# A hybrid encoder layer on one core: the fourth renewed block's remainder taken on GpSimd instead of VectorE

## The chip, the cores and the metric

The kernel runs on one core of a Trainium2 chip. A core has a matrix engine (TensorE, PE in the profile, with its weight loads as PEld), three engines for elementwise work (VectorE = DVE, ScalarE = ACT, GpSimd = POOL) and SyncE (SP), which here only issues transfers between main memory and the on-chip buffer (SBUF). Each engine carries out its own instructions strictly in order and waits at the first one whose inputs are not there. Matmul results go to eight banks of accumulator memory (PSUM), which DVE and ACT read.

The metric is the time of one execution in microseconds (us) on the device. Before the change it is 2638.22 us, the median of three runs (2640.26, 2638.22 and 2636.32).

## The reference, cut to what matters

```python
def hybrid_layer(x, norm_mix_w, w_in, ...):
    h = rmsnorm(x, norm_mix_w)
    proj = einsum("btd,dc->btc", h, w_in)
    u_b, u_c, u_h, z, xbc, dt_raw = split(proj, SPLITS)
    y_a = short_conv_mixer(u_b, u_c, u_h, short_conv_w)     # y = B * conv3(C * h)
    y_b = ssd_mixer(z, xbc, dt_raw, ...)                    # conv, chunked scan, gate, norm
    x = x + einsum("btc,cd->btd", concat([y_a, y_b]), w_out)
    h = rmsnorm(x, norm_mlp_w)
    hid = square(relu(einsum("btd,df->btf", h, w_up)))
    return x + einsum("btf,fd->btd", hid, w_down)

def reference(x, ...):          # x: 1 x 2048 x 1024 float32, one layer, d_ff 4096
    return rmsnorm(hybrid_layer(x, ...), final_norm_w)
```

## The kernel before, in words

**Three matmuls for one.** All products are float32. A block of activations is kept as two halves: `uh`, the value rounded by a cast on ACT, and `ul`, the remainder (value minus `uh`), a subtraction on DVE. Weights are split in the same way into `whi` and `wlo` (`split_w`, L98 to L102: cast on ACT at L100, remainder on DVE at L101). A product is then uh·whi + ul·whi + uh·wlo (L281, L282, L283). A matmul works on a 128x512 tile of activations.

**Seven products for eight.** The four large products (input projection, output projection, MLP up and MLP down) are done in pairs of output columns with seven block products instead of eight; `chain` (L250) issues them in the order b11, t1, t2, b21, t3, b22, t4, twelve matmuls each where four blocks are summed. Their activations are not only the four blocks but sums of them: each of four input groups k = 0 to 3 has four *places* i = 0 to 3. `WHERE` (L193) says which product reads which place: b11 and t1 read place 0, t2 and b21 place 1, t3 and b22 place 2, t4 place 3. Places 0 to 2 are 128x1024 (two tiles), place 3 is 128x512. Products accumulate in the banks px, py and pw, and the next product on a bank waits for the copy that takes the last one out: pw starts from a copy of px after b11 (L288, ACT); t3 goes into px only after ACT has copied t2's result away (`s2<-px`, L746 in the projection, L890 in the MLP).

**Renewing the places.** Three times a product's whole set of places gives way to the next set, which was stored in main memory. It happens inside the last pair that uses the old set: as soon as a place's last product of that pair is issued, the new blocks of this place are cast and their remainders taken, while the later products of the pair still read the other places. `refresh` (L424) does so in the projection's first half, at the end (new blocks `rb` loaded from `hm_d`; called site A below) and at the end of the MLP's first half (`rb` from `hn_d`; site C). `refill` (L979) does so at the end of the MLP's second half, for the first step of the down product (`rh` from `hid_d`; site D). Both call `settle` (L348) after t1, b21, b22 and t4 with i = 0, 1, 2, 3, and right behind it issue the loads of the following place. Those loads go into a ring of four buffers (`uraw`, L201), one for each k, so the load of place i+1 of group k waits until cast and remainder of place i of group k have read the buffer. A fourth use (site B, L1589 and L1598, entry of the MLP) settles places 0 and 1 from tiles that are in SBUF already, with no load behind it. Elsewhere (`stow` at L866, `refill` of one group during the down product) `settle` gets one group only, so k is 0 there.

**What sets the order.** Python code is run once to record the instructions; a scheduler, which goes by its own estimates of durations, then decides for each engine the order in which they stand. So a change of one instruction's engine can move others. SP issues every load and store of these places in one queue: one that must wait holds all behind it. At site D this queue also carries the weights of the down product (`wraw<-w_down`, L972), the stores of the hidden blocks (`hid_d<-...`, L880 and L881) and the sixteen loads of the tiles to which the down product is added (`acc<-x1_d`, L997); an addition on DVE (L1037) frees a bank of the down product once its `acc` tile has landed. GpSimd has next to nothing to do in this kernel: copies of two or three columns for the convolutions, and nine multiplications at the very end (L1133).

Of the kernel before, what the change touches and what calls it, by code (L numbers as in the profile page):

```python
# [11 lines left out]
F32 = mybir.dt.float32  # L12
F32R = mybir.dt.float32r
AF = mybir.ActivationFunctionType
ALU = mybir.AluOpType
# [25 lines left out]
def trunk(ctx: ExitStack, tc: tile.TileContext, x, w_in, w_dt, w_out, w_up, w_down, cvec, hrow, out):  # L41
    nc = tc.nc
# [37 lines left out]
        out=tri, in_=tri, compare_op=ALU.is_ge, fill=0.0, base=0, pattern=[[1, P]], channel_multiplier=-1  # L80
# [115 lines left out]
    class Seven:  # L196
# [149 lines left out]
            return got  # L346

        def settle(self, places, i, got):  # L348
            for p, t in zip(places, got):
                p[i] = self.place(i)  # L350
                t = t[:, 0:1] if i == 3 else t
                nc.scalar.copy(p[i][0], t)  # L352
                nc.vector.tensor_tensor(out=p[i][1], in0=t, in1=p[i][0].bitcast(F32), op=ALU.subtract)

        def last_sums(self):
            for p, t4 in zip(self.places, self.t4s):
# [1309 lines left out]
```

## Time and profile before

| | |
|---|---|
| three runs | 2640.26, 2638.22, 2636.32 us; median 2638.22 |
| profiled execution | 2635.81 us, span 2633.6 us, mean granted TensorE clock 0.997 |
| instructions on DVE / on POOL | 2634 / 98 |
| main memory | 537 MB moved, mean 204 GB/s |

The profile is of one further execution; its span is the time from its first to its last instruction, 2.2 us less than its own time. "Busy" is the share of the span in which an engine works. The chain that ended last is followed back from the last instruction and says, for each stretch of the span, which engine or wait it hung on. A row of the timeline has the start, the duration, the engine and line, the operation with output<-inputs and shape, and in brackets how long the engine had been idle and which instruction or transfer ended that. SPq rows are transfers as SP issues them: their duration is the issuing, not the transfer.

### The profile page before, as it was taken

Reading aid. Unit: us, or ns where it says so; the run is one execution under the profiler, and the core shown is the slowest. Engines: PE = TensorE matmul, PEld = TensorE weight load, DVE = VectorE, ACT = ScalarE, POOL = GpSimd, SP = SyncE. Lnnn points to the kernel's source line nnn. Section 1 sums busy time; section 2 is a strip of 40 time slices with the busy share of each in tenths; the row PEclk is TensorE's granted clock in tenths of the full one; section 3 lists DMA queues with packets and bytes.
Section 4 is the critical chain, followed back from the end, with each engine's and each line's share of the span. In section 5 each row is a group of like instructions: output and inputs, shape, how many; then the busy total and the mean of one; then the engine's idle time right before and its main releaser. Section 6 shows DMA issues by size and latency. Waiting matters only on the chain.

```text
span 2633.6 us, 33784 instructions
## 1 busy us (share of the span) xinstructions
PE 2603.1 (99%) x12136; PEld 2142.1 (81%) x12136; DVE 1919.1 (73%) x2634; ACT 1456.4 (55%) x2211; POOL 55.6 (2%) x98
## 2 busy tenths in 40 slices
PE   9999999999999999999999999999999999999998
PEld 7888888788888888787888888888887888888887
DVE  7977867777778777768677775644448877888985
ACT  6654345776667675857336555655555444444443
POOL 0010000000000000000000000000000000000001
PEclk9999999999999999999999999999999999999999
DMA  3645735555555587867656786765558544665762
GB/s 147 205 168 190 273 144 197 187 165 172 175 169 164 162 283 255 264 210 228 204 195 238 264 314 235 281 211 200 187 197 288 159 150 153 213 208 166 250 208 77
DMA packets 252168, 536.97 MB, mean 204 GB/s; under 512 B 26208, under 2 KB 93024, under 8 KB 252000
## 3 DMA queue, kind: packets, MB, share of 16 engines
q1 hardware_dynamic: 251856, 534.29, 60.7%
q8 instruction: 95, 1.56, 0.2%
q14 instruction: 73, 0.60, 0.1%
q10 hardware_dynamic: 144, 0.52, 0.1%
HBM read 354.89 MB, written 179.83 MB: 203 GB/s over the span
## 4 chain that ended last, share of the span: by engine, by line
PE 65%; issue 25%; ACT 4%; DMA 4%; DVE 2%; POOL 0%; SPq 0%; POOLq 0%; DVEq 0%; ACTq 0%
PE px L281 10%; PE px L282 9%; PE px L283 9%; PE py L281 5%; PE py L282 5%; PE py L283 5%; PE pm L113 4%; PE pm L114 4%; PE pm L115 4%; PE pw L281 2%; PE pw L282 2%; PE pw L283 2%; PE yd L1315 1%; PE yo L1312 1%; ACT dec L1292 1%
## 5 line engine op out<-in xcount | busy, mean ns | idle before, releaser
L281 PE MATMUL px<-uh,whi 128*128 128x512 f32 x1672 | 656.2, 392 | 8.3 <-DVE acc L1037 3.8
L283 PE MATMUL px<-uh,wlo 128*128 128x512 f32 x1672 | 651.6, 390 | 0.0
L282 PE MATMUL px<-ul,whi 128*128 128x512 f32 x1672 | 651.4, 390 | 0.0
L281 PEld LDWEIGHTS px<-uh,whi 128*128 128x128 f32 x1672 | 314.3, 188 | 81.1 <-DVE acc L1037 5.0
L101 DVE TENSOR_TENSOR wlo<-wraw,whi 128x1024 fp32r<-128x1024 f32 x214 | 222.7, 1041 | 203.6 <-ACT whi L100 203.4
L283 PEld LDWEIGHTS px<-uh,wlo 128*128 128x128 f32 x1672 | 314.2, 188 | 66.2 <-issue 0.2
L100 ACT CAST whi<-wraw 128x1024 fp32r<-128x1024 f32 x214 | 194.3, 908 | 313.8 <-PE px L282 224.2
L282 PEld LDWEIGHTS px<-ul,whi 128*128 128x128 f32 x1672 | 314.4, 188 | 63.5
L100 ACT CAST whi<-s 128x1024 fp32r<-128x1024 f32 x210 | 220.1, 1049 | 229.1 <-PE py L282 90.7
L281 PE MATMUL py<-uh,whi 128*128 128x512 f32 x836 | 327.3, 392 | 4.3 <-DVE acc L1037 3.1
L282 PE MATMUL py<-ul,whi 128*128 128x512 f32 x836 | 325.8, 390 | 0.0
L283 PE MATMUL py<-uh,wlo 128*128 128x512 f32 x836 | 325.5, 390 | 0.0
L101 DVE TENSOR_TENSOR wlo<-s,whi 128x1024 fp32r<-128x1024 f32 x210 | 255.5, 1217 | 73.1 <-ACT whi L100 71.5
L113 PE MATMUL pm<-uh,whi 128*128 128x512 f32 (+1 forms) x648 | 251.0, 388 | 0.1
L114 PE MATMUL pm<-ul,whi 128*128 128x512 f32 (+1 forms) x648 | 248.2, 383 | 0.3 <-DVE ul L211 0.2
L115 PE MATMUL pm<-uh,wlo 128*128 128x512 f32 (+1 forms) x648 | 247.9, 383 | 0.0
L281 PEld LDWEIGHTS py<-uh,whi 128*128 128x128 f32 x836 | 156.9, 188 | 39.1 <-DVE acc L1037 3.5
L283 PEld LDWEIGHTS py<-uh,wlo 128*128 128x128 f32 x836 | 157.0, 188 | 33.0 <-DVE wlo L101 0.2
L282 PEld LDWEIGHTS py<-ul,whi 128*128 128x128 f32 x836 | 157.0, 188 | 32.1
L352 ACT CAST uh<-rh 128x1024 fp32r<-128x1024 f32 (+1 forms) x128 | 120.5, 944 | 82.1 <-PE py L283 61.9
L281 PE MATMUL pw<-uh,whi 128*128 128x512 f32 x418 | 163.3, 391 | 0.7 <-ACT pw L288 0.7
L283 PE MATMUL pw<-uh,wlo 128*128 128x512 f32 x418 | 162.8, 389 | 0.0
(241 smaller groups left out, 3794.4 us busy)
## 6 DMA issues: line engine op xcount, KB each, us to landing
hid_d<-e SPq DMA_DIRECT2D x96, 512.0 KB, 3.9
rh<-hid_d SPq DMA_DIRECT2D x96, 512.0 KB, 4.4
wraw<-w_in SPq DMA_DIRECT2D x68, 512.0 KB, 3.8
wraw<-w_down SPq DMA_DIRECT2D x104, 256.0 KB, 3.5
wraw<-w_up SPq DMA_DIRECT2D x48, 512.0 KB, 4.3
dec<-rd_d SPq DMA_DIRECT2D x32, 512.0 KB, 5.0
wraw<-w_out SPq DMA_DIRECT2D x32, 512.0 KB, 4.7
x_d<-xt SPq DMA_DIRECT2D x64, 256.0 KB, 3.3
```

Of the source, the lines that this page charges most:

```text
L100: nc.scalar.copy(hi, raw)
L101: eng.tensor_tensor(out=lo, in0=raw, in1=hi.bitcast(F32), op=ALU.subtract)
L113: nc.tensor.matmul(out, whi, hi, start=(k == 0), stop=False)
L114: nc.tensor.matmul(out, whi, lo, start=False, stop=False)
L115: nc.tensor.matmul(out, wlo, hi, start=False, stop=(k == nk - 1))
L281: nc.tensor.matmul(p, hi, h[0], start=not seeded and k == 0, stop=False, **kw)
L282: nc.tensor.matmul(p, hi, h[1], start=False, stop=False, **kw)
L283: nc.tensor.matmul(p, lo, h[0], start=False, stop=(k == len(g) - 1), **kw)
L352: nc.scalar.copy(p[i][0], t)
L1292: nc.scalar.activation(dec[:, i], dec[:, i], AF.Relu, bias=t["a"][:, i : i + 1], scale=-1.0)
L1312: nc.tensor.matmul(yo[:, j * L : (j + 1) * L], state[:, j * P : (j + 1) * P], cT, start=True, stop=True)
L1315: nc.tensor.matmul(yd[(i % 2) * 64 : (i % 2) * 64 + 64, (i // 2) * L : (i // 2 + 1) * L], byhead(t["xdt"])[:, i, :], t["dec"][:, i % 2 * 4 ...
```

## The change

In `settle` the remainder of the fourth group (k = 3) is taken by GpSimd instead of VectorE. Cast, shapes and arithmetic are the same; the other three groups stay.

```diff
         def settle(self, places, i, got):
-            for p, t in zip(places, got):
+            for k, (p, t) in enumerate(zip(places, got)):
                 p[i] = self.place(i)
                 t = t[:, 0:1] if i == 3 else t
                 nc.scalar.copy(p[i][0], t)
-                nc.vector.tensor_tensor(out=p[i][1], in0=t, in1=p[i][0].bitcast(F32), op=ALU.subtract)
+                eng = nc.gpsimd if k == 3 else nc.vector
+                eng.tensor_tensor(out=p[i][1], in0=t, in1=p[i][0].bitcast(F32), op=ALU.subtract)
```

The lines behind it move by one (L353 becomes L354, L997 becomes L998). Fourteen instructions go from DVE to POOL. On GpSimd these are the first six of them, four at site A (places 0 to 3) and two at B (places 0 and 1); four each at C and D follow, of the same shapes as at A:

```order
L354 TENSOR_TENSOR ul0_3646<-rb_3616,uh0_3645 128x1024
L354 TENSOR_TENSOR ul1_3708<-rb_3655,uh1_3707 128x1024
L354 TENSOR_TENSOR ul2_3768<-rb_3717,uh2_3767 128x1024
L354 TENSOR_TENSOR ul3_3810<-rb_3777,uh3_3809 128x512
L354 TENSOR_TENSOR ul0_12067<-first_11891,uh0_12066 128x1024
L354 TENSOR_TENSOR ul1_12155<-nb_11892,uh1_12154 128x1024
```

The scheduler also moves other instructions at these sites and nowhere else. No instruction is added or dropped. At site C this is ACT's order before, around the fourth place (`uh3`) of the new blocks; `s5` and `s2` are the copies of t1's and t2's results, `whi_14755` is a later weight:

```order
L352 CAST uh3_14663<-rb_14637 128x512
L100 CAST whi_14755<-wraw_14706 128x1024
L352 CAST uh3_14667<-rb_14639 128x512
L352 CAST uh3_14671<-rb_14641 128x512
L890 COPY s5_14725<-py_14712 128x512
L890 COPY s2_14739<-px_14691 128x512
L896 ACTIVATE e0_14688<-pw_14704 128x512
L352 CAST uh3_14675<-rb_14643 128x512
```

The same stretch on ACT with the change:

```order
L352 CAST uh3_14663<-rb_14637 128x512
L891 COPY s5_14725<-py_14712 128x512
L100 CAST whi_14755<-wraw_14706 128x1024
L352 CAST uh3_14667<-rb_14639 128x512
L352 CAST uh3_14671<-rb_14641 128x512
L352 CAST uh3_14675<-rb_14643 128x512
L891 COPY s2_14739<-px_14691 128x512
L897 ACTIVATE e0_14688<-pw_14704 128x512
```

The cast of the last renewed block (`uh3_14675`) stands ahead of the copy `s2<-px` now, and behind it before. At site A the two were in this order already; there the last cast (`uh3_3809`) and a 128x1024 weight cast (`whi_3947`) change places. ACT at site A before:

```order
L352 CAST uh3_3805<-rb_3775 128x512
L100 CAST whi_3947<-wraw_3853 128x1024
L352 CAST uh3_3809<-rb_3777 128x512
L746 COPY s5_3886<-py_3873 128x512
L746 COPY s2_3915<-px_3838 128x512
```

and with the change:

```order
L352 CAST uh3_3805<-rb_3775 128x512
L352 CAST uh3_3809<-rb_3777 128x512
L100 CAST whi_3947<-wraw_3853 128x1024
L747 COPY s5_3886<-py_3873 128x512
L747 COPY s2_3915<-px_3838 128x512
```

So the weight cast now lies between the last block's cast and the two copies. PE at site A takes t4 of the ending pair in one piece ahead of the next pair's b11, where before five matmuls of b11 came first; at site D it does the same with all twelve of b11.

At site D, SP's queue before, behind the last load of the fourth place (`wraw_17166` and `wraw_17167` are weights of the down product's third step, `e0`, `e1` and `t4` the last hidden blocks that are stored):

```order
L989 DMA rh_16953<-hid_d0_3_116 128x512
L972 DMA wraw_17166<-w_down 128x128 x2
L972 DMA wraw_17166<-w_down 128x384
L880 DMA hid_d1_15_144<-e0_16760 128x1024
L880 DMA hid_d1_15_144<-e1_16761 128x1024
L881 DMA hid_d1_15_144<-t4_16989 128x512
L972 DMA wraw_17166<-w_down 128x384
L972 DMA wraw_17167<-w_down 128x128 x2
L972 DMA wraw_17167<-w_down 128x384
L997 DMA acc_17003<-x1_d0_77 128x512
```

The same part of SP's queue with the change:

```order
L990 DMA rh_16953<-hid_d0_3_116 128x512
L881 DMA hid_d1_15_144<-e0_16760 128x1024
L881 DMA hid_d1_15_144<-e1_16761 128x1024
L882 DMA hid_d1_15_144<-t4_16989 128x512
L973 DMA wraw_17051<-w_down 128x256 x2
L973 DMA wraw_17166<-w_down 128x128 x2
L998 DMA acc_17003<-x1_d0_77 128x512
```

The second half of the second step's weights (`wraw_17051`), which stood ahead of the fourth place's loads before, moved behind the store of `t4_16989`. The sixteen `acc` loads now come ahead of the weights in pieces of 384, which follow behind them. On ACT at site D the copy `pw<-px` of the down product's first step moved from right behind the cast of `uh2_16931` to behind the cast of `uh3_16973`, the first block of the fourth place, and the cast of the second step's first weight (`whi_17096`) from ahead of the last two casts of `uh3` to behind them.

## The prediction, made before the changed kernel ran

> **What bounds the kernel.** I read the page's busy line and its chain of waits first, then what PE waited for, then the timelines around the places that the change touches.
>
> ```profile
> PE 2603.1 (99%) x12136; PEld 2142.1 (81%) x12136; DVE 1919.1 (73%) x2634; ACT 1456.4 (55%) x2211; POOL 55.6 (2%) x98
> PE 65%; issue 25%; ACT 4%; DMA 4%; DVE 2%; POOL 0%; SPq 0%; POOLq 0%; DVEq 0%; ACTq 0%
> ```
>
> PE is busy 99% of the span, and the chain that ended last lies on PE or its issuing for 90%. DVE is the fuller of the helpers, yet only 2% of the chain hangs on it. A time saved on DVE is worth something only where PE waits for DVE. The list of PE's waits (engine, line, what it waited for: total us, times, longest) says where:
>
> ```profile
> PE px L281 <- DVE acc L1037: 3.8, 6, 1.4
> PE py L281 <- DVE acc L1037: 3.1, 1, 3.1
> PE px L281 <- ACT s L746: 1.3, 1, 1.3
> ```
>
> The 3.1 us wait (down product) is at site D, the 1.3 us one (ACT's copy in front of t3) at site A. No wait for a remainder `ul` of a renewed block is among the larger ones. So the gain that the change can bring directly is small, and the question is what lies behind the moved instructions.
>
> **The moved instruction.** Fourteen subtractions leave DVE, eleven of 128x1024 and three of 128x512. The groups by form (count | busy us, mean ns of one | idle before) give DVE's price, and the only larger GpSimd instructions of this kernel:
>
> ```profile
> L353 DVE TENSOR_TENSOR ul<-rb,uh 128x1024 fp32r<-128x1024 f32 x24 | 28.4, 1222 | 7.2 <-ACT uh L352 7.2
> L353 DVE TENSOR_TENSOR ul<-rb,uh 128x512 fp32r<-128x512 f32 x8 | 5.4, 690 | 3.0 <-ACT uh L352 3.0
> L1133 POOL TENSOR_TENSOR acc<-acc,rstd 128x256 f32<-128x256 f32 x6 | 4.4, 768 | 12.8 <-ACT rstd L186 12.8
> L1133 POOL TENSOR_TENSOR acc<-acc,rstd 128x512 f32<-128x512 f32 x3 | 4.0, 1363 | 1693.6 <-ACT rstd L186 1693.6
> ```
>
> DVE is relieved of 11 x 1.22 + 3 x 0.69 = 15.5 us. On GpSimd 128x512 costs 1.36 us and each further 256 columns 1.363 - 0.768 = 0.6 us, so a 128x1024 remainder is estimated at 1.36 + 2 x 0.6 = 2.55 us. No row has one: from below it is DVE's 1.22, from above twice 1.36 = 2.7. I take 2.55, which lies near the upper, GpSimd's own row.
>
> Whether GpSimd can start at once is the second unknown. Its small copies show it (first one alone, then one beside DVE, with DVE's rows):
>
> ```profile
> 146.38 0.19 POOL L700 COPY halo<-buf 128x3 f32<-128x3 f32 x1 [32.64 <-DVE buf L749]
> 178.04 2.23 POOL L732 COPY ch<-halo_s 128x2 f32<-128x2 f32 x1 [8.49 <-DVE cacc L704]
> ...
> 177.80 0.69 DVE L214 TENSOR_TENSOR s<-wraw 128x512 f32<-128x512 f32 x1
> 178.40 0.69 DVE L214 TENSOR_TENSOR s<-wraw,s 128x512 f32<-128x512 f32 x1
> 179.00 1.22 DVE L101 TENSOR_TENSOR wlo<-wraw,whi 128x1024 fp32r<-128x1024 f32 x1
> ```
>
> A copy of 0.19 us took 2.23 and ended at 180.27, just behind three back-to-back DVE subtractions (end 180.22). So GpSimd waits here while DVE reads two SBUF tiles, from 0 up to 2.23 - 0.19 = 2.0 us, until DVE has a gap. I take no more than the end of the DVE instruction in progress, because at A and C the remainder that left DVE makes the gap itself; 2.0 us stays as the other end.
> The Trainium skill, "SBUF — State Buffer", section "Who interferes with whom", speaks against this change: a DVE instruction with two SBUF inputs and a GpSimd instruction that reads SBUF exclude each other, and the later one "fully blocks" for the whole instruction. The trace agrees in kind; by the letter of the rule GpSimd would lose at most the rest of one 1.22 us instruction, which is the forecast's case, while the row at 178.04 waited through three.
>
> **Site A.** Rows of ACT, then DVE, SP and PE:
>
> ```profile
> 461.39 1.04 ACT L352 CAST uh<-rb 128x1024 fp32r<-128x1024 f32 x1
> 467.19 1.06 ACT L100 CAST whi<-wraw 128x1024 fp32r<-128x1024 f32 x1 [0.78 <-PE px L282]
> 469.65 0.62 ACT L352 CAST uh<-rb 128x512 fp32r<-128x512 f32 x1 [1.41 <-DMA rb<-hm_d]
> 470.66 0.59 ACT L746 COPY s<-px 128x512 f32<-128x512 f32 x1
> 461.30 2.40 DVE L353 TENSOR_TENSOR ul<-rb,uh 128x1024 fp32r<-128x1024 f32 x2
> 463.72 0.32 SPq L344 DMA_DIRECT2D rb<-hm_d  x1
> 456.55 0.50 PE L281 MATMUL px<-uh,whi 128*128 128x512 f32 x1 [0.88 <-DVE eb L749]
> 461.55 0.50 PE L281 MATMUL py<-uh,whi 128*128 128x512 f32 x1 [0.40 <-ACT eb L784]
> 471.30 0.50 PE L281 MATMUL px<-uh,whi 128*128 128x512 f32 x1 [1.26 <-ACT s L746]
> ```
>
> The cast of place 2, k = 3 ends at 462.43, its remainder on DVE at 463.70, and 0.02 us later SP issues the load of place 3, k = 3 into the freed buffer. ACT then stands still until this block lands (469.65), casts it, makes the two copies, and t3 starts 0.05 us after the second. So load, cast and copy set t3's start. On GpSimd the remainder starts when DVE's k = 2 one ends (461.30 + 1.21 = 462.51) and ends at 465.06: 1.35 us later. In ACT's new order the weight cast of 467.19, which lay inside ACT's wait, comes between the last cast and the copies: 1.06 us. t3 moves by 1.35 + 1.06 = 2.4 us. If the landing does not move with the issue (it took 5.9 us, so other traffic may set it), 1.06 is left; with GpSimd 2.0 us late it is 4.4.
>
> PE's earlier waits here (0.88 and 0.40) can go, since DVE and ACT have less ahead of `eb`; that only lengthens the stall at t3, to 1.26 + 1.28 + 2.4 = 4.9 us. A long stall has a price of its own, as the windows at site D show (window: us, then busy per engine, then PEclk):
>
> ```profile
> 2008.00:2012.00 4.00, 0.90 (x4) 0.43 (x4) 1.77 (x4) 0.41 (x1) 0.00 (x0) 1.00 0.93 270
> 2012.00:2016.00 4.00, 4.00 (x12) 2.86 (x11) 0.68 (x1) 0.00 (x0) 0.00 (x0) 0.57 0.99 361
> 2016.00:2020.00 4.00, 4.00 (x19) 3.29 (x18) 2.18 (x4) 1.06 (x1) 0.00 (x0) 1.00 1.05 387
> ```
>
> After the 3.10 us stall the granted clock was 0.57 for 4 us: 4 x 0.43 = 1.7 us lost. The 1.26 us stall at A has no such trace now. I add 1.7: **A +4.1**, bounds +1.1 and +6.1.
> The Trainium skill, "TensorE: Matmul & The Clock Gate", Part 1, puts the idle window that halves the clock at about 3.4 us; here 3.10 was enough, so the measurement decides, and by either number A's stall pays.
>
> **Site B.** No load hangs on these two remainders.
>
> ```profile
> 1364.00:1383.00 19.00, 19.00 (x85) 15.54 (x84) 15.58 (x18) 9.96 (x11) 0.00 (x0) 1.00 0.31 113
> ```
>
> PE is busy for all 19 us and the places are cast well before use: **B 0**, bounds 0 and +1 (a remainder 1.3 us later in front of its first product).
>
> **Site C.**
>
> ```profile
> 1689.69 1.05 ACT L352 CAST uh<-rb 128x1024 fp32r<-128x1024 f32 x1
> 1695.16 0.58 ACT L890 COPY s<-px 128x512 f32<-128x512 f32 x1
> 1696.45 0.62 ACT L352 CAST uh<-rb 128x512 fp32r<-128x512 f32 x1 [0.21 <-DMA rb<-hn_d]
> 1689.57 3.02 DVE L353 TENSOR_TENSOR ul<-rb,uh 128x1024 fp32r<-128x1024 f32 x3
> 1692.02 0.32 SPq L344 DMA_DIRECT2D rb<-hn_d  x1
> 1695.80 0.50 PE L281 MATMUL px<-uh,whi 128*128 128x512 f32 x1
> ```
>
> The copy ends at 1695.74 and t3 starts at 1695.80: there is no slack. The last block landed at 1696.45 and its cast stood behind the copy; now it stands ahead. Even with the landing unmoved the copy starts at 1696.45 + 0.62, ends 0.58 later at 1697.65, and t3 comes 1.9 us later than now. The load is issued when the remainder of place 2, k = 3 is done; on GpSimd that is 1690.79 (end of DVE's k = 2 one) + 2.55 = 1693.34, 1.3 us after the 1692.02 of now. **C +3.2**, bounds +1.9 and +5.2, with a clock loss of up to 1.7 on top (the stall is about 3.1 us, the edge; not counted).
>
> **Site D.**
>
> ```profile
> 1990.56 0.58 ACT L288 COPY pw<-px 128x512 f32<-128x512 f32 x1
> 1997.27 0.60 ACT L352 CAST uh<-rh 128x512 fp32r<-128x512 f32 x1
> 1995.39 0.39 PE L281 MATMUL px<-uh,whi 128*128 128x512 f32 x1
> 2003.72 0.32 SPq L881 DMA_DIRECT2D hid_d<-t  x1
> 2006.55 7.54 SPq L997 DMA_DIRECT2D acc<-x_d  x12
> 2010.16 0.69 DVE L1037 TENSOR_TENSOR acc<-pw,acc 128x512 f32<-128x512 f32 x1 [1.04 <-DMA acc<-x_d]
> 2011.56 0.50 PE L281 MATMUL py<-uh,whi 128*128 128x512 f32 x1 [3.10 <-DVE acc L1037]
> ```
>
> The `acc` loads go out 2.8 us after the store of t4 because four groups of weights stand between; the first addition waits for them, and PE for the additions. With t4 of the last pair ahead of b11, its block is ready up to 2.5 us earlier (twelve matmuls, at 19 in 4 us), and the loads go out in front of the weights. Against this, the copy `pw<-px`, at 1990.56 now, comes behind the cast of 1997.27, so t2 (now 1995.39) waits some 3 us; and the fourth place's last load, which waits for GpSimd, now stands ahead of store, weights and `acc` in SP's queue, while the second step's second weights are issued only behind that store. PE had 3.10 us to wait in any case, so what comes first is absorbed. I estimate the additions 2.3 us earlier: **D -2.3**; bounds -4.8 (3.10 and the clock's 1.7 both gone) and +1.5 (the weights of the second step land after PE wants them).
>
> **Sum.** 4.1 + 0 + 3.2 - 2.3 = +5.0 us: 2640.8 by the profiled execution's 2635.81, which is 2.4 under the median of the runs; on the median's footing 2638.2 + 5.0 = **2643.2 us**. The bounds add to -1.8 and +15.5.
>
> **Rivals.** (1) *GpSimd is kept out* (slower): at A, C and D it finds no gap and starts 2.0 us late as at 178.04. It decides from the point where the stall at C passes 3.1 us and pays the clock too: A 6.1, C 5.2 + 1.7, D about 0 (the SP queue loses what it gained), +13.0, 2651. For it: DVE's rows at C run back to back. Against: the missing remainder leaves a gap of 1.2 us. (2) *The loads' landing does not move and D gives all*: A 1.1, C 1.9, D -4.8: -1.8, 2636; for it the 5.9 us landing at A, against it SP's queue at D with one more wait at its head. (3) *All is covered*, 2638: speaks for it that only 2% of the chain is DVE's; against, that ACT's orders at A and C put a block which lands last ahead of a copy that PE waits for. That the change does not do what it says is excluded by GpSimd's list of instructions.
>
> **Chances.** Forecast 0.47, rival 1 0.27, rival 2 0.16, rival 3 0.10. A measurement of this kernel tells about 0.2%, 5.3 us, from no change: under 2632.9 is faster, over 2643.5 slower. The forecast lies just inside the border and is split 0.32 same, 0.15 slower; rival 1 is slower; rival 2 gives 0.10 to faster (where the clock also holds at A) and 0.06 to same; rival 3 is same. Faster 0.10, same 0.48, slower 0.42. The range goes from rival 2 less the 2 us by which the runs differ, 2634, to rival 1 with as much, 2653.
>
> **What would show it.** GpSimd's `ul<-rb` and `ul<-rh` at 2.5 us and starting when DVE's k = 2 remainder ends; PE waiting for `s` (L747) 3 to 5 us at A and about 3 us for `s` (L891) at C, with a granted clock under 0.7 behind the first; at D a new wait of PE near 1995 and a smaller one for `acc` (L1038). It is wrong if t3 at C starts without a wait, if GpSimd takes well over 3 us for one remainder, or if a wait for weights takes over at D.

## The result, and the profile after

The changed kernel took **2645.41 us** (median of seven executions, 2641.24 to 2650.44), the kernel before 2639.32 us (seven, 2636.32 to 2640.59) on the same chip: a ratio of 1.0025, 95% interval 1.0015 to 1.0035. In the run at the end of the experiments it was 2644.63 (ten) against 2636.6 (thirteen), 1.0034 [1.0023, 1.0045]. The change costs 0.25% in the first comparison and 0.34% in the second, 6.1 and 8.0 us. The forecast was 2643.2 us, 5.0 us more than before: the sign and about the size came out, but not by the terms that were put down. By the border that the prediction drew (over 2643.5) the kernel is slower, which had a chance of 0.42; "same" had 0.48.

The page of the profiled execution after (2645.41 us, span 2643.7), busy line and chain that ended last:

```profile
PE 2607.1 (99%) x12136; PEld 2143.6 (81%) x12136; DVE 1919.2 (73%) x2620; ACT 1454.7 (55%) x2211; POOL 90.6 (3%) x112
...
PE 64%; issue 25%; DMA 4%; ACT 4%; DVE 2%; POOL 1%; SPq 0%; POOLq 0%; DVEq 0%; ACTq 0%
```

Fourteen instructions have left DVE, and DVE is as busy as before: 1919.2 against 1919.1 us, where the prediction relieved it of 15.5. The work moved and the same amount of standing came in: beside the fourteen remainders on GpSimd, DVE's instructions took 15.1 us longer in all than the median of the same form before (16.4 in the other profile of this kernel), from 0 to 2.2 us for each remainder. The groups by form of POOL (count | busy us, mean ns of one | idle before) show what one remainder takes there:

```profile
L354 POOL TENSOR_TENSOR ul<-rb,uh 128x1024 fp32r<-128x1024 f32 x6 | 16.0, 2668 | 343.9 <-PE px L282 291.6 <-ACT uh L352 52.3
...
L354 POOL TENSOR_TENSOR ul<-rh,uh 128x1024 fp32r<-128x1024 f32 x3 | 7.6, 2540 | 296.6 <-ACT uh L352 296.6
...
L354 POOL TENSOR_TENSOR ul<-first,uh 128x1024 fp32r<-128x1024 f32 x1 | 3.5, 3462 | 457.5 <-ACT uh L352 457.5
```

The estimate of 2.55 us holds for the means at A, C and D (2.54 and 2.67; single ones take 2.40 to 3.24). At B it is 3.5: the first one there starts at 1371.14, just behind the start of a DVE subtraction of 1.22 us (1371.13), and is 1.06 us longer than the shortest, most of that subtraction. The list of PE's waits (engine, line, what it waited for: total us, times, longest):

```profile
PE px L281 <- ACT pw L288: 4.7, 2, 4.4
...
PE px L281 <- ACT s L891: 3.6, 2, 2.3
...
PE px L281 <- ACT s L747: 1.8, 2, 1.4
```

The 3.1 us wait for `acc` is gone. In its place stand 4.4 us for `pw` (site D) and 2.3 us for `s` at L891 (site C). The wait at A (L747) is 1.4, hardly more than the 1.26 of before. To give each site its own price, I took from each trace the time between two fixed matmuls of PE ahead of and behind the site (from the 1950th to the 2240th for A, 6600 to 6760 for B, 7900 to 8120 for C, 9240 to 9600 for D), minus the same in the profile of before, in us:

```
                              A       B       C       D
before, itself              63.8    37.8    50.2    90.7
after                      +0.10   +0.26   +2.87   +2.73
A alone                    +2.83   -0.77   +0.22   -0.91
C alone                    +0.26   -0.34   +3.99   +0.13
D alone                    -0.69   -0.51   -0.02   +2.13
C, copy first              +0.06   -0.06   +0.09   -0.82
D, pw first                +0.71   -1.11   +0.24   +2.71
D, pw and weights first    +0.72   -0.41   -0.04   +5.41
acc loads first            -0.61   -0.41   +0.16   +0.40
D, three places            +0.79   -0.12   +0.28   +0.71
after, once more           +0.34   +1.23   +1.93   +1.91
```

The rows below "after" are the experiments. A site that a kernel leaves as it was says how far such a number can be trusted: within 0.3 at C, 0.8 at A, 0.9 at D. Outside the four sites, where no instruction changed its place, single profiles differ more: the stretch between A and B took 3.1 us longer than before in the profile of after and 3.0 us less in the other profile of the same kernel. PE's waits for `xtok` (L1289 before), most of them in this stretch, sum to 4.2 us before, 5.0 and 1.6 in these two, and the granted clock was halved there for one period of 3.4 us, for two, and not at all. The site numbers add to 6.0 and 5.4 us, while the medians differ by 6.1 and 8.0; what is above the sites' sum is not assigned to any step here.

### The profile page after: what moved, and what is told of

Read it like the earlier page. It is cut to its first block, busy times and chain, and to the rows that moved or that the text cites. A ratio compares the mean times of both kernels' runs of the same rounds, so it can differ in the third digit from the quotient of the medians.

```text
span 2643.7 us, 33785 instructions
## 1 busy us (share of the span) xinstructions
PE 2607.1 (99%) x12136; PEld 2143.6 (81%) x12136; DVE 1919.2 (73%) x2620; ACT 1454.7 (55%) x2211; POOL 90.6 (3%) x112
## 4 chain that ended last, share of the span: by engine, by line
PE 64%; issue 25%; DMA 4%; ACT 4%; DVE 2%; POOL 1%; SPq 0%; POOLq 0%; DVEq 0%; ACTq 0%
PE px L281 9%; PE px L282 9%; PE px L283 9%; PE py L281 5%; PE py L283 5%; PE py L282 5%; PE pm L113 4%; PE pm L114 4%; PE pm L115 4%; PE pw L281 2%; PE pw L283 2%; PE pw L282 2%; DMA dec<-rd_d 1%; PE yd L1316 1%; PE yo L1313 1%
```

## The experiments

### One site at a time

The three uses of `settle` with loads behind them get a name, and GpSimd takes the fourth remainder at one site only:

```diff
-        def settle(self, places, i, got):
+        def settle(self, places, i, got, site=""):
...
+                eng = nc.gpsimd if k == 3 and site in ('A',) else nc.vector
```

(`'C'` and `'D'` in the other two.)

> Only site A (the projection's renewal, rb from hm_d) takes its fourth remainder on GpSimd; B, C and D as before, so that the order of instructions is that of the changed kernel at A and that of before everywhere else. In the changed kernel's profile PE stood 1.5 to 2 us ahead of before from A on. Theory 'order' (the scheduler's new order decides, not GpSimd's slowness): the same here, t3 of the next pair starts about 1.6 us earlier than before (the 0.88 and 0.40 us waits of before shrink), time 1 to 2 us under before. Theory 'lock' (GpSimd and VectorE shut each other out, and the remainder is 2.5 us instead of 1.22): the gain at A was chance, time 0 to 4 us over before, as my prediction had it (+4.1).

> Only site C (the MLP's renewal, rb from hn_d) on GpSimd. Both theories: PE waits about 2.3 us for the copy s<-px in front of t3, time 2 to 4 us over before; this is the base for the next run. If PE does not wait there, what the changed kernel lost at C was not C's own.

> Only site D (the MLP's renewal for the down product, rh from hid_d) on GpSimd. In the changed kernel PE waited 4.4 us for the copy pw<-px at D and the 3.10 us wait for acc was gone; the clock was halved for two periods of 3.4 us where before had one. Theory 'order': the same wait of 4 to 5 us for pw, no long wait for acc, time +0 to +4. Theory 'lock': a wait of VectorE's e (L894) first in the chain, two VectorE instructions of more than 2 us beside GpSimd's, time +2 to +5.

Measured: A alone 2639.49 us against 2637.7, ratio 1.0003 [0.9993, 1.0014]; C alone 2640.84, 1.0012 [1.0002, 1.0022]; D alone 2639.52, 1.0008 [0.9999, 1.0017]. The three add to 0.23% beside 0.25% and 0.34% for the whole. Each is known to about 0.1% only, so nothing asks for sites that cost more together than alone, but a share of 0.1% of that kind, or of B, is not excluded. A alone is 2.8 us longer by the profile, which goes with the second theory (0 to 4 us over before) and against the first (1 to 2 under); C came as both theories had it; at D the wait for `pw` of the one and the long DVE instructions of the other both came, so that this run does not part them. At D the sign of the prediction is the wrong one. PE with D alone:

```profile
2000.23 0.63 PE L281 MATMUL px<-uh,whi 128*128 128x512 f32 x1 [4.27 <-ACT pw L288]
...
2009.61 0.50 PE L281 MATMUL pw<-uh,whi 128*128 128x512 f32 x1 [0.66 <-ACT pw L288]
```

t2 waits 4.27 us for the copy `pw<-px`, and no wait for `acc` follows nearby. At C the wait is the predicted one, for `s`:

```profile
1696.67 0.62 ACT L352 CAST uh<-rb 128x512 fp32r<-128x512 f32 x1 [2.03 <-DMA rb<-hn_d]
1697.20 0.58 ACT L891 COPY s<-px 128x512 f32<-128x512 f32 x1
...
1697.83 0.50 PE L281 MATMUL px<-uh,whi 128*128 128x512 f32 x1 [2.17 <-ACT s L891]
```

ACT stands still for 2.03 us until the last block lands, with the copy that PE needs queued behind the cast. The stretch is 4.0 us longer here and 2.9 in the profile of after: here the trace also has the clock halved for 3.4 us from 1698.2, which costs half of that, 1.7.

### Site C: the order, or GpSimd's slower remainder?

GpSimd keeps its remainder at C, but a dependence that only orders the two (`behind(later, first)`) puts the copy `s2<-px` back ahead of the last cast on ACT:

```diff
+                cast = nc.scalar.copy(p[i][0], t)
+                kept[site, i, k] = cast
+                eng = nc.gpsimd if k == 3 and site in ('C',) else nc.vector
...
-                nc.scalar.copy(s[name], pm)
+                c = nc.scalar.copy(s[name], pm)
+                if (h, q, name) == (1, 0, 's2'):
+                    behind(kept['C', 3, 3], c)
```

> Site C on GpSimd as in the run before it, but the copy s<-px of the next pair is put back ahead of the cast of the last renewed block on ScalarE, where it stood before the change (an order edge, no wait); nothing else of VectorE, GpSimd or SyncE moves. Theory 'order': PE's wait in front of t3 falls from 2.3 to at most 0.4 us and the time is that of before within 1 us. Theory 'lock': the load and the remainder stay late and VectorE stays held, so at least 1.5 us of the loss at C remains.

Measured: 2637.13 us, ratio 0.9998 [0.9989, 1.0007]; the stretch at C is 0.09 us longer than before. The timeline of this kernel, whose lines are numbered a little higher (L357 is the cast, L360 the remainder, L897 the copy):

```profile
1690.53 2.63 POOL L360 TENSOR_TENSOR ul<-rb,uh 128x1024 fp32r<-128x1024 f32 x1 [5.92 <-ACT uh L357]
1690.84 2.88 DVE L219 TENSOR_TENSOR e<-e,e 128x512 f32<-128x512 f32 x1
...
1694.57 0.58 ACT L897 COPY s<-px 128x512 f32<-128x512 f32 x1
...
1696.11 0.62 ACT L357 CAST uh<-rb 128x512 fp32r<-128x512 f32 x1 [0.95 <-DMA rb<-hn_d]
```

The remainder on GpSimd is as slow as ever, DVE is held beside it (2.88 us for an instruction of 0.69), the block lands after the copy, and PE waits for none of it. At C the whole cost hangs on the place of one copy in ACT's order: with the copy first, the later block and the held DVE cost nothing.

### Site D: what holds the copy into pw?

First, the copy `pw<-px` is put ahead of the third cast of the third place (`uh2`):

```diff
+                        c = nc.scalar.copy(pm[gi]["w"], pm[gi]["x"])
+                        if "now" in kept:
+                            behind(kept.pop("now"), c)
...
+                if n == 0:
+                    kept["now"] = kept["D", 2, 2]
```

> Site D alone on GpSimd as in e3, but the copy pw<-px of the down product's first step is put ahead of the cast of the third place's third block on ScalarE (an order edge); SyncE's queue keeps the second step's second weights behind the store of t4. In e3 PE waited 4.3 us for this copy. Theory 'one gate' (the copy behind the casts is what site D lost): the wait for pw goes and site D, +2.1 us against before in e3, falls by 3 us or more. Theory 'two gates' (the second step's weights, issued behind the fourth place's last load, which waits for GpSimd, come too late as well): the wait for pw goes, but PE then waits 3 us or more for whi (L100) or the copy behind it near 2010, and site D stays within 1.5 us of e3.

Measured: 2637.27 against 2637.34 us, 1.0002 [0.9993, 1.0011]; yet the stretch at D is 2.71 us longer than before. The wait moved instead of going away (PE in this kernel, L286 to L288 are its matmul lines):

```profile
1997.33 0.50 PE L286 MATMUL px<-uh,whi 128*128 128x512 f32 x1 [1.71 <-ACT pw L293]
...
2004.52 0.50 PE L288 MATMUL px<-uh,wlo 128*128 128x512 f32 x1 [1.00 <-DVE wlo L101]
...
2010.05 0.50 PE L286 MATMUL py<-uh,whi 128*128 128x512 f32 x1 [2.00 <-ACT whi L100]
```

1.71 us for the copy instead of 4.27, and 1.00 and 2.00 us for weights of the next products. That the stretch stays near that of D alone is what "two gates" had expected, though the wait for `pw` is not gone and none of the later ones reaches 3 us. The median of the runs shows no cost here; its interval reaches up to 0.11%, 2.9 us. The next kernel takes one more cast (`kept["D", 2, 1]`) behind the copy; with it the order puts the weights earlier too:

> As e6, but with the copy one cast further ahead, where the scheduler also takes the second step's weights ahead of the fourth place's last loads in SyncE's queue, and the acc loads behind the third step's first weights. Theory 'two gates': both waits are gone, PE waits for acc again as before (2 to 3 us), site D within 1 us of before. Theory 'lock' (VectorE held by GpSimd is what costs): site D stays 2 us over before, as in e3, since GpSimd does the same four remainders.

Measured: 2643.30 us, 1.0022 [1.0012, 1.0032], D +5.41: neither theory's number. The wait for the copy is down to 0.77 us, PE stands 3.12 us for the low half of a weight, and the clock is halved for 6.8 us from 2009.1 on:

```profile
1999.34 0.50 PE L286 MATMUL px<-uh,whi 128*128 128x512 f32 x1 [0.77 <-ACT pw L293]
...
2008.65 0.50 PE L288 MATMUL px<-uh,wlo 128*128 128x512 f32 x1 [3.12 <-DVE wlo L101]
```

So at D the copy is only the first of several gates. Behind it come the weights of the first two steps, whose casts and remainders stand in the same queues as the renewed places. Neither of these two orders brings D under the time of before.

How much of D is the order, and how much GpSimd holding DVE? The next kernel leaves the remainder of place 1 (i = 1) on DVE and gives GpSimd the three others at D:

```diff
+                eng = nc.gpsimd if k == 3 and i != 1 and site == 'D' else nc.vector
```

> Site D on GpSimd as in e3, but the second place's remainder goes back to VectorE; the copy pw<-px still stands behind the cast of the fourth place's first block. In e3 two VectorE subtractions took 4.56 us together (2.35 alone) while that GpSimd remainder ran, and ScalarE then stood still for 2.25 us until VectorE's e (L894). Theory 'lock adds to the order': PE's wait for pw falls from 4.3 to about 2 to 3 us. Theory 'order alone': it stays at 4 us or more, since the copy is held by the loads of the fourth place.

Measured: 2638.59 us, 1.0008 [0.9999, 1.0017]; the wait for `pw` falls from 4.27 to 3.11 us, just above the 2 to 3 that "lock adds to the order" had, and the stretch from +2.13 to +0.71; the medians of the runs (2638.59 and 2639.52) don't tell the two kernels apart. First the timeline of the changed kernel, where these rows are as with D alone, then that of this one, around the place:

```profile
1993.65 4.56 DVE L354 TENSOR_TENSOR ul<-rh,uh 128x1024 fp32r<-128x1024 f32 x2
...
1994.67 2.46 POOL L354 TENSOR_TENSOR ul<-rh,uh 128x1024 fp32r<-128x1024 f32 x1 [7.42 <-ACT uh L352]
1998.85 0.63 ACT L897 ACTIVATE e<-e 128x512 f32<-128x512 f32 x1 [2.25 <-DVE e L894]
...
2005.99 0.58 ACT L288 COPY pw<-px 128x512 f32<-128x512 f32 x1
```

```profile
1987.31 3.48 DVE L354 TENSOR_TENSOR ul<-rh,uh 128x1024 fp32r<-128x1024 f32 x3
...
1991.43 0.63 ACT L897 ACTIVATE e<-e 128x512 f32<-128x512 f32 x1 [0.24 <-DVE e L894]
...
1992.44 2.35 DVE L354 TENSOR_TENSOR ul<-rh,uh 128x1024 fp32r<-128x1024 f32 x2
...
1998.38 0.58 ACT L288 COPY pw<-px 128x512 f32<-128x512 f32 x1
```

Two remainders on DVE take 2.35 us alone (the row at 1992.44, of the next place), and 4.56 where GpSimd's one starts near the end of the first: 2.21 more, nearly the 2.46 of GpSimd's instruction. For this place that is a bad trade: DVE does all three remainders itself in 3.48 us (the row at 1987.31), 1.08 us sooner than two beside GpSimd. ACT waits 2.25 us for DVE's `e` behind the 4.56, and with it everything in ACT's queue up to the copy into pw; here it waits 0.24. Without this one hold the copy's wait is 1.16 us shorter. This is not the hold alone, since the scheduler also took one cast (1.04 us) ahead of that `e` on ACT here. The other 3.1 us I put down to the order of the casts ahead of the copy, as the two kernels before suggest (waits of 1.71 and 0.77 with the copy further ahead); no run shows this part by itself.

### Did the acc loads gain by going ahead of the weights?

DVE everywhere, as before, but the weights of the third step go out behind the first step's `acc` loads in SP's queue:

```diff
+                            if step is STEPS[2]:
+                                kept["n"] = kept.get("n", 0) + 1
+                                if kept["n"] > 3:
+                                    behind(c, kept["acc"])
```

> Nothing on GpSimd, all as before, but in SyncE's queue at D the acc loads are put ahead of the third step's last weights (from its fourth piece on), which had cost before its 3.10 us wait by my reading. If that reading is right: the wait for acc shrinks from 3.1 to at most 1 us, the half-clock period near 2012 goes, and site D takes 2 to 4 us less than before, time 2634 to 2636 against 2638. If the acc tiles' memory is what comes late, or the third step's weights then do: no gain, a wait for whi or wlo in place of the one for acc.

Measured: 2639.29 us, 1.001 [1.0001, 1.002], D +0.40. The timeline of this kernel (L1008 issues the `acc` loads):

```profile
2000.76 0.32 SPq L888 DMA_DIRECT2D hid_d<-t  x1
...
2002.12 10.76 SPq L1008 DMA_DIRECT2D acc<-x_d  x16
...
2009.26 0.50 PE L286 MATMUL py<-uh,whi 128*128 128x512 f32 x1 [3.77 <-DVE acc L1050]
```

The loads go out 1.4 us behind the store instead of 2.8, and PE waits 3.77 us for them, not 3.10. Counted from the 9240th matmul, the first load is issued 2.4 us earlier than before and lands 0.3 us earlier: from issue to landing the shortest takes 5.3 us and the median 5.8, where before it was 3.6 and 6.0. The product that waits starts 0.3 us earlier too; the wait is longer only because PE arrives there 1.0 us earlier. So the reading that the weights ahead of the `acc` loads cost PE that wait has fallen.

### The changed kernel once more

Unchanged code; open was the size of A, which the profiles of after (+0.1) and of A alone (+2.8) gave differently.

> The changed kernel once more, for a second profile of its three sites; what is open is the size of the first: the profile of after has its stretch 0.1 us longer than before, the one with that site alone 2.8 us. That the late cast alone is paid there (theory): stretch A between 0 and 3 us longer, C 2.5 to 4 longer with TensorE waiting 2.1 to 2.4 us for s (L891), D 2 to 3 longer with a wait of 4.2 to 4.5 us for pw (L288); the ratio to before between 1.0015 and 1.0035. That the first site costs what the prediction gave it (rival): stretch A over 4 us longer, with a wait of TensorE there of 3 us or more.

Measured: 2644.63 against 2636.6 us, 1.0034 [1.0023, 1.0045]. A is +0.34, with a wait of 1.7 us for `s`: the theory's side, and far from 4. C is +1.93 with a wait of 1.65, and D +1.91 with one of 4.40; the first is less than the theory had asked, the last two numbers are at its edge or in it. The reason for C shows in the timeline (GpSimd's remainder of place 2, the load behind it, the block's cast, t3):

```profile
1690.14 2.73 POOL L354 TENSOR_TENSOR ul<-rb,uh 128x1024 fp32r<-128x1024 f32 x1 [6.44 <-ACT uh L352]
...
1692.89 0.32 SPq L344 DMA_DIRECT2D rb<-hn_d  x1
...
1695.82 0.62 ACT L352 CAST uh<-rb 128x512 fp32r<-128x512 f32 x1 [1.77 <-DMA rb<-hn_d]
...
1696.97 0.50 PE L281 MATMUL px<-uh,whi 128*128 128x512 f32 x1 [1.65 <-ACT s L891]
```

The load is issued 0.02 us after the remainder, as the prediction said, but lands 2.93 us later; before it took 4.43 (1692.02 to 1696.45). That a load issued later finds less ahead of it would explain this; no run shows it.

## Why the forecast was right, and where its steps were not

**What bounds the kernel.** Right: PE is the bound, busy 99% of the span, and DVE's part of the chain is 2% before and after. What a gain on DVE is worth was not put to the test, as DVE gained nothing.

**GpSimd's price.** 2.55 us was taken, 2.54 and 2.67 measured in the mean. That GpSimd is held no longer than one DVE instruction is about right too. At A the remainder of place 2 starts 0.24 us before DVE's k = 2 row ends (461.48, against 460.49 + 1.23, in the rows of site A below) and takes 2.52 us, 0.1 more than the shortest, 2.40. At C it takes 3.24 and 2.73 us in the two profiles and at D 2.76, so the hold is 0 to 0.8 us there and not the 2.0 of rival 1. The lock between the two engines was seen from one side only: GpSimd's own waiting got a price, DVE's waiting for GpSimd got none. It is up to 2.2 us for one remainder where DVE has work with two inputs in SBUF meanwhile, and over the whole kernel it ate the 15.5 us that DVE was to save. Where DVE's instruction takes one input from PSUM it is not held: `eb<-px,s` and `ea<-py,s` (L750) took 0.68 us each at 453.64 and 454.24, inside GpSimd's row of 453.46 to 455.98. The Trainium skill, "SBUF — State Buffer", section "Who interferes with whom", says of the port pair that DVE shares with GpSimd that whoever issues first has it for the whole instruction and that the other "fully blocks"; the rows at 1993.65 and 1994.67 agree, and there it is DVE that loses.

**Site A: +4.1 forecast, +0.1 and +0.3 measured** (+2.8 with A alone). The mechanism of ACT's order was right, its sum was not. The timeline of after:

```profile
460.49 1.23 DVE L354 TENSOR_TENSOR ul<-rb,uh 128x1024 fp32r<-128x1024 f32 x1
461.48 2.52 POOL L354 TENSOR_TENSOR ul<-rb,uh 128x1024 fp32r<-128x1024 f32 x1 [5.50 <-ACT uh L352]
...
458.00 6.35 SPq L344 DMA_DIRECT2D rb<-hm_d  x4
...
467.10 0.62 ACT L352 CAST uh<-rb 128x512 fp32r<-128x512 f32 x1 [2.06 <-DMA rb<-hm_d]
467.63 1.04 ACT L100 CAST whi<-wraw 128x1024 fp32r<-128x1024 f32 x1
...
469.69 0.50 PE L281 MATMUL px<-uh,whi 128*128 128x512 f32 x1 [1.42 <-ACT s L747]
```

From the start of the last cast to t3 it is 2.59 us, before 1.65: the weight cast's term, put at 1.06, measures 0.94. What failed is "t3 moves by 1.35 + 1.06": the last load goes out at 464.03 (the end of the row of four issues less one of 0.32), right behind the remainder, and has landed 3.07 us later, where before it took 5.9. Counted from the 1950th matmul the load is issued 1.1 us later than before and lands 1.8 us earlier, and t3 starts 0.9 us earlier, where the forecast had it 2.4 later (in the other profile of this kernel the three are 1.6 later, 1.45 earlier and 0.5 earlier). The forecast's lower bound (1.1) let the landing stand still; that it could come earlier was not in it, and both measured numbers lie under that bound. With it fell the stall of 4.9 us: it is 1.4 and 1.7, and the 1.7 us for the halved clock behind it were never paid. Also the earlier waits there fell from 0.88 and 0.40 to one of 0.59, which pays most of the weight cast back. That the stretch is no shorter than before comes for the most part from a wait further on, which the forecast does not have (PE's waits of after, whole span):

```profile
PE pc L678 <- DVE dts L672: 0.9, 1, 0.9
```

It lies at 500.3 and stands in every kernel with A on GpSimd (0.9 and 1.0 us in the changed kernel, 1.1 with A alone); in no other kernel does PE wait there. What makes `dts` late is not shown.

**Site B: 0 forecast**, +0.3 and +1.2 measured in a stretch that moves by up to 1.1 in kernels that leave it alone. Right, as far as this can tell.

**Site C: +3.2 forecast, +2.9 and +1.9 measured.** Right in mechanism, shown by the run with the copy put first, which undoes all of it. Counted from the 7900th matmul, t3 starts 3.05 and 2.2 us later than before in the two profiles. Of the two parts of the sum the cast ahead of the copy (1.9) came in full: 1.8 in both. The later issue was put at 1.3; the load is issued 2.7 and 1.9 us later, since GpSimd's remainder starts later and is held longer than was taken, and lands 1.25 and 0.4 us later. So the first profile agrees with the forecast part by part, and in the second the transfer made up most of the delay, as at A.

**Site D: -2.3 forecast, +2.7 and +1.9 measured.** The wrong sign. The predicted wait for `pw` came (4.4 us, put at 3). The wait of 3.1 us for `acc` went, but not because the additions came earlier. SP's queue and the first addition in after:

```profile
2009.75 0.32 SPq L882 DMA_DIRECT2D hid_d<-t  x1
2010.12 2.90 SPq L973 DMA_DIRECT2D wraw<-w_down  x4
2013.06 10.80 SPq L998 DMA_DIRECT2D acc<-x_d  x16
...
2018.03 0.68 DVE L1038 TENSOR_TENSOR acc<-pw,acc 128x512 f32<-128x512 f32 x1
```

Four issues of weights still stand between the store of t4 and the `acc` loads, as before, and the loads go out 3.3 us behind the store (2.8 before). Counted from the 9240th matmul the store goes out at 28.9 us (29.2 before, where its block was to be ready up to 2.5 us earlier), the first `acc` load at 32.2 and in the other profile 32.0 (32.05), and the first addition starts at 37.2 and 36.3 (35.7). So the 2.3 us that the additions were to gain did not come at all; they are 0.6 to 1.5 us later. PE no longer waits for them because it comes later itself. PE's waits of 1985 to 2060 us, before (without the 3.1 for `acc` at py, shown earlier):

```profile
PE px L281 <- DVE acc L1037: 1.2, 1, 1.2
PE py L281 <- ACT whi L100: 0.7, 1, 0.7
PE pw L281 <- ACT pw L288: 0.7, 1, 0.7
PE px L281 <- DVE e L893: 0.2, 1, 0.2
```

and after:

```profile
PE px L281 <- ACT pw L288: 4.4, 1, 4.4
PE px L281 <- DVE acc L1038: 2.2, 2, 1.8
PE pw L281 <- ACT pw L288: 0.7, 1, 0.7
PE px L281 <- DVE e L894: 0.5, 1, 0.5
```

5.9 us in all before, 7.8 after: 1.9 of the measured 1.9 to 2.7. In the profile of after the clock was also halved for 6.8 us instead of 3.4, 1.4 us of them inside PE's wait, which by half the difference in running time is an estimated 1.0 us more; in the other profile it was 3.4 us as before. Two steps failed. The first is "I estimate the additions 2.3 us earlier". The second is "what comes first is absorbed", with that gain taken beside it, and it would have failed even with early additions. A wait that comes first delays PE's own arrival at the product that needs the additions, and this product starts at the later of two times, PE's arrival and the additions' end. With the additions early and a wait of 3 us ahead, PE's arrival decides: by the prediction's own numbers 3.0 - 3.1 is about 0, not -2.3. The 1.3 us by which the wait for `pw` is longer than the 3.1 that went are GpSimd's hold on DVE, mostly (1.16 by the run with three places, with the cast that moved there). The rest is the wait for `acc` at px (1.2 to 2.2) and for `e` (0.2 to 0.5), less the wait for weights that went (0.7).

The errors at A (too high by some 4) and at D (too low by 4 to 5) nearly cancelled in the sum of +5.0. So the forecast came out by luck, through two errors of opposite sign, and only C was right by its reasons. Rival 2 was nearer at A, with a landing that does not move, and had D's gain wrong; rival 1 had its price for A and C from a hold of 2.0 us, of which 0 to 0.8 came.

**Not settled.** Why A alone is 2.8 us longer at A, with waits of 1.9 for `s` and 0.9 for `pw`, while the whole change is 0.1 and 0.3; its last load is issued 1.3 to 1.9 us later there than with the whole change. Whether A costs anything is open by the medians too (1.0003, with an interval that holds 1). At D, how the cost divides between the order and the hold is known only by the one kernel in which both moved a little. And which part of the spread of the changed kernel (2641 to 2651 us) belongs to its sites: its traces show halved clocks at other places in one execution than in the next.

## What to carry to other kernels

Before moving an instruction to an idle engine, list what its new duration does to the order on all the others: here one swap on ACT, a cast that waits for a load ahead of the copy that TensorE waits for, cost 2 to 4 us, and putting that one copy first gave it all back. Two waits in a row on one engine are joined by a maximum, not a sum: take the time at which each of the inputs is there, and the engine's own arrival with the earlier wait in it. And an instruction with two SBUF inputs on VectorE beside one on GpSimd has to be priced from both sides, since the one that starts later can stand for nearly the whole length of the other (2.2 of 2.46 us here).

## What the runs showed of the hardware that was not expected

**VectorE loses what GpSimd takes.** At D two 128x1024 subtractions took 4.56 instead of 2.35 us, and a 128x512 instruction with two SBUF inputs 2.73 to 2.91 instead of 0.69, each beside one GpSimd subtraction of 2.4 to 3.0 us. The standing is counted as busy time in the profile. ScalarE's 128x512 casts at the same time kept their 0.62 us.

**The halved clock comes in whole periods.** The windows of after behind the wait at D (window: us, then busy per engine, then PEclk, DMA share, GB/s):

```profile
2004.00:2008.00 4.00, 1.38 (x3) 1.16 (x4) 3.96 (x4) 3.24 (x7) 2.76 (x1) 0.65 0.79 284
2008.00:2012.00 4.00, 4.00 (x11) 3.06 (x10) 2.93 (x5) 1.47 (x3) 0.93 (x1) 0.50 0.88 306
2012.00:2016.00 4.00, 4.00 (x19) 3.17 (x17) 1.69 (x4) 0.34 (x1) 0.35 (x1) 1.00 0.87 288
```

Apart from the last 12 us of the span, the clock is halved in these traces for 3.4 us or for 6.8 (from 2005.2 on in this one). What brings it on isn't the stall's length alone: 4.38 us gave 6.8 here and 4.40 gave 3.4 in the other profile of the same kernel; 2.17 us at C gave one period, 2.27 us none. The periods lie on a grid: from one change of the clock to the next there were always whole multiples of 3.413 us, in all eleven traces (in this one 321, 1, 33, 1, 230, 2 and 183 of them), so that equal stalls fall differently into it. That this decides is not shown. The Trainium skill, "TensorE: Matmul & The Clock Gate", Part 1, gives windows of about 3.4 us, which is the length seen.

**A later load need not land later.** Counted from the fixed matmul ahead of each site, the last block's load at A was issued 1.1 us later than before and landed 1.8 us earlier (3.07 us instead of 5.9), and at C it was issued 2.7 us later and landed 1.25 us later, in the other profile 1.9 and 0.4 us. The first `acc` load, issued 2.4 us earlier, landed 0.3 us earlier. That the landing hung on what else was under way (a DMA share of 0.8 to 0.9 in the windows above, at D) would fit, but no run here takes it apart.
